# Macaron 1 with four pairs of PSUM banks, a head of products before each group's downs, and token sums on VectorE

## The chip, the cores and the metric

The kernel runs on one core of a Trainium2 chip. The metric is device time in microseconds, the median of several runs. Inside the core, TensorE (PE) multiplies and accumulates into PSUM, VectorE (DVE), ScalarE (ACT) and GpSimd (POOL) work on SBUF and PSUM, and the SP queue issues nearly all loads. PSUM has eight banks of 512 fp32 columns on 128 partitions.

## The reference

One layer of a hybrid trunk with D = 1024, 512 latent tokens x and 256 context tokens ctx (768 token columns), fp32:

```
u = rms_norm(s, g) * (1 + scale) + shift
s = s + 0.5 * gate * ((silu(u @ w_gate) * (u @ w_up)) @ w_down)      # macaron 1
... input projection; Hyena long convolution and differential attention; output projection, gated residual ...
... the same half-step once more (macaron 2); final rms_norm; out: x
```

w_gate and w_up are 1024 x 2816, w_down 2816 x 1024. Shift, scale and gate come from silu(c) @ ada_w + ada_b (9 vectors of 1024, for c and, in the first stages, for c_ctx).

## The kernel before

All large products run as three TensorE products of split operands: x = hi + lo, hi a copy rounded to fp32r and lo the rest; hi·hi + hi·lo + lo·hi (`mm3`, L252 to L255). So each weight and each activation needs a cast on ACT (hi) and a subtraction on DVE (lo). Tokens lie along the columns (TT = 768, HT = 384 is half of them), features along the partitions.

`macaron1` (L592) does the first half-step. Its 2816 hidden features are 22 f-tiles of 128. The first NP0 = 4 f-tiles are multiplied plainly (banks g0x and u0x, 768 columns in a pair of banks); Silu on ACT (L624), multiply on DVE (L625), split. The other 18 are worked on in pairs, by a scheme of the Strassen kind: a unit is the gate (m = 0) or the up matrix (m = 1) of one pair of f-tiles, and seven products j = 0 to 6 in place of eight, each of 4 x 3 = 12 matmuls with 384 columns (`product`, L731), into four accumulators: two bank pairs, called ab and cd. The weights of products 1, 2, 3 and 6 are sums of blocks (`sums_of`, L714), those of the tokens are the sums t1 to t4, made once by `token_sums` (L639; subtractions in L645) during the downs of group 0. `after_product` (L744) empties the accumulators: u is product 0 saved, further additions (L755, L760, L764, L774 to L779) give the four quarters, m = 0 ends in Silu, m = 1 in the multiply and in the split for the downs.

f-tiles come in groups (GROUPS1). After each group the downs: for each of 8 output tiles d one product with 512 latent columns and one with 256 context columns, each of 3 matmuls per f-tile, added to the stream s by DVE (`after_down`, L804). The context downs of the last group are done later, one by one between other work (the part of `macaron1` after its `yield`).

`order` is the list of all products and downs. Each step i runs its matmuls, then casts the weights of step i + 8 (9 slots; `cast` L721, `low` L726), empties the step before, and moves on something else: during group 0's downs the token sums, otherwise steps of `ada_steps` (L325), paced by PACE. These steps accumulate the later modulation vectors on DVE (L337, L339: a 128 x 1024 block of ada_w times a column of c, 70 and more of them); `ada_sum` then sums over partitions by transposing on PE (L319) and reducing on DVE (L320), and `finish_mods` (L260 to L266) adds the bias. Some steps lie between the first four f-tiles (`side`).

PSUM is one pool for the whole program: two pairs (tag "two") and four single banks ("one", downs and modulation sums). The tile framework orders each engine's instructions by the order of the code, with priorities; buffers are waited for when they come round. SP issues the loads in program order into two raw blocks of 1 MB.

```
t = bank1(f"dn0{g}{d}{strm}")[:, :n]                                        # L798
PACE = {"p": 0.2, 2: 0.35, 4: 1.6}                                          # steps per product, per down of 2 or 4 f-tiles
```

## Time and profile before

| | |
|---|---|
| three runs | 1353.21, 1356.2, 1358.03 us; median 1356.2 |
| the profiled execution | 1357.22 us, of which the span is 1355.5 |
| busy: PE / DVE / ACT / POOL | 1259.9 / 952.3 / 506.4 / 208.0 us |
| macaron 1 from the end of u03 to the last group's context downs | 144.40 to 611.08 us |

The span runs from the first to the last instruction on the core; the time of a run also has what lies around it. An engine's busy time is the sum of its instructions, where PE's overlap in a pipeline (a matmul's duration is longer than the distance to the next one's start). A wait is idle time of an engine put down to the instruction that released it.

### The profile page before, as it was taken

How to read it: one execution, taken by the hardware profiler on the slowest of the kernel's cores; microseconds unless marked ns; L12 is line 12 of the kernel's file. 1: busy time of each engine (PE TensorE's matmuls, PEld its weight loads, DVE VectorE, ACT ScalarE, POOL GpSimd, SP SyncE). 2: the span in 40 equal slices, each digit the busy share in tenths (PEclk: the TensorE clock that was granted, in tenths of full speed). 3: DMA queues.
4: the chain of work that ended last, by engine and by line, in shares of the span. 5: the costliest groups of instructions: out<-in, count | busy, mean ns of one | idle time of the engine just before them, and what ended most of it. 6: DMA issues, size and time to landing. Idle time of an engine off the chain costs nothing. (4 is left out here: it accounts for less than half of the span.)

```text
span 1355.5 us, 17492 instructions
## 1 busy us (share of the span) xinstructions
PE 1259.9 (93%) x6928; PEld 1107.7 (82%) x6928; DVE 952.3 (70%) x1453; ACT 506.4 (37%) x805; POOL 208.0 (15%) x180
## 2 busy tenths in 40 slices
PE   5899899999999999998988999888899999999996
PEld 2479788999999989987877998777788888888886
DVE  6988999778968986758598567897874333333346
ACT  5652232341331332434333345575442232222233
POOL 3630200000000000010035156464110000000001
PEclk8899899999999999999999999899899999999999
DMA  7636133222425551221412111202462322322321
GB/s 284 228 117 224 42 100 118 93 94 78 141 93 159 173 196 44 82 93 35 150 63 94 64 48 53 88 32 93 140 221 79 123 90 84 118 89 82 125 63 63
DMA packets 28370, 147.69 MB, mean 109 GB/s; under 512 B 3264, under 2 KB 3648, under 8 KB 17792
## 3 DMA queue, kind: packets, MB, share of 16 engines
q1 hardware_dynamic: 26432, 140.28, 30.9%
q0 software_dynamic: 1856, 6.29, 1.3%
q8 instruction: 54, 0.88, 0.3%
q14 instruction: 28, 0.23, 0.0%
HBM read 141.32 MB, written 5.24 MB: 108 GB/s over the span
## 5 line engine op out<-in xcount | busy, mean ns | idle before, releaser
L239 DVE TENSOR_TENSOR arena_r<-arena_f,arena_r 128x1024 fp32r<-128x1024 f32 (+5 forms) x201 | 210.8, 1059 | 156.2 <-ACT arena_r L238 153.0
L238 ACT CAST arena_r<-arena_f 128x1024 fp32r<-128x1024 f32 (+5 forms) x215 | 186.6, 879 | 353.8 <-PE gu L254 126.9
L721 ACT CAST arena_r<-arena_f 128x512 fp32r<-128x512 f32 (+1 forms) x174 | 105.8, 610 | 273.4 <-PE dn L254 102.3
L254 PE MATMUL gu<-arena_r 128*128 128x512 f32 (+1 forms) x416 | 155.5, 374 | 2.6 <-POOL arena_r L390 2.4
L253 PE MATMUL gu<-arena_r 128*128 128x512 f32 (+1 forms) x416 | 155.3, 375 | 0.7 <-ACT arena_r L238 0.6
L255 PE MATMUL gu<-arena_r 128*128 128x512 f32 (+1 forms) x416 | 155.2, 373 | 0.6 <-DVE arena_r L239 0.6
L726 DVE TENSOR_TENSOR arena_r<-arena_f,arena_r 128x512 fp32r<-128x512 f32 (+1 forms) x174 | 118.7, 686 | 34.3 <-ACT arena_r L721 32.7
L741 PE MATMUL cd<-arena_r 128*128 128x384 f32 x684 | 124.4, 335 | 5.3 <-DVE arena_f L779 5.3
L741 PEld LDWEIGHTS cd<-arena_r 128*128 128x128 f32 x684 | 118.6, 188 | 7.2 <-DVE arena_f L779 7.0
L253 PE MATMUL dn<-arena_r,arena_r 128*128 128x256 f32 (+1 forms) x328 | 107.6, 335 | 8.8 <-DVE arena_f L320 6.0
L239 POOL TENSOR_TENSOR arena_r<-arena_f,arena_r 128x1024 fp32r<-128x1024 f32 (+1 forms) x14 | 31.3, 2246 | 497.3 <-ACT arena_r L238 496.3
L254 PE MATMUL dn<-arena_r,arena_r 128*128 128x256 f32 (+1 forms) x328 | 107.6, 332 | 0.0
L255 PE MATMUL dn<-arena_r,arena_r 128*128 128x256 f32 (+1 forms) x328 | 107.1, 330 | 0.0
L339 DVE SCALAR_TENSOR_TENSOR arena_f<-arena_f,cs 128x1024 f32<-128x1024 f32 x70 | 90.4, 1302 | 10.7 <-DMA arena_f<-in_ada 10.4
L254 PEld LDWEIGHTS gu<-arena_r 128*128 128x128 f32 x416 | 80.0, 192 | 16.5 <-POOL arena_r L390 2.8
L253 PEld LDWEIGHTS gu<-arena_r 128*128 128x128 f32 x416 | 79.6, 192 | 15.6 <-issue 1.2
L741 PE MATMUL ab<-arena_r 128*128 128x384 f32 x492 | 91.0, 336 | 0.6 <-ACT arena_r L721 0.6
L255 PEld LDWEIGHTS gu<-arena_r 128*128 128x128 f32 x416 | 79.9, 192 | 13.8 <-DVE arena_r L239 0.8
L741 PEld LDWEIGHTS ab<-arena_r 128*128 128x128 f32 x492 | 85.6, 189 | 1.0 <-ACT arena_r L721 0.9
L253 PE MATMUL dn<-arena_r 128*128 128x512 f32 (+1 forms) x232 | 85.7, 370 | 0.0
L254 PE MATMUL dn<-arena_r 128*128 128x512 f32 (+1 forms) x232 | 85.7, 369 | 0.0
L255 PE MATMUL dn<-arena_r 128*128 128x512 f32 (+1 forms) x232 | 85.6, 369 | 0.0
(291 smaller groups left out, 2675.5 us busy)
## 6 DMA issues: line engine op xcount, KB each, us to landing
arena_f<-in_wgu SPq DMA_DIRECT2D x46, 1024.0 KB, 5.1
arena_f<-in_ada SPq DMA_DIRECT2D x62, 512.0 KB, 3.8
arena_f<-in_wd SPq DMA_DIRECT2D x11, 1024.0 KB, 5.1
arena_f<-in_win SPq DMA_DIRECT2D x10, 1024.0 KB, 4.9
arena_f<-in_wout SPq DMA_DIRECT2D x8, 1024.0 KB, 4.9
arena_e<-in_ada SPq DMA_DIRECT2D x10, 512.0 KB, 7.1
arena_f<-in_wd SPq DMA_DIRECT2D x4, 896.0 KB, 4.6
arena_f<-in_wd SPq DMA_DIRECT2D x4, 768.0 KB, 4.2
```

The costliest lines, as they stand in the source:

```text
L238: S.copy(hi, src)
L239: eng.tensor_tensor(out=lo, in0=src, in1=hi.bitcast(F32), op=ALU.subtract)
L253: T.matmul(out_, lh, rh, start=start, stop=False)
L254: T.matmul(out_, lh, rl, start=False, stop=False)
L255: T.matmul(out_, ll, rh, start=False, stop=stop)
L339: V.scalar_tensor_tensor(out=acc, in0=w, scalar=sc, in1=acc, op0=ALU.mult, op1=ALU.add)
L721: S.copy(slots[i % NS][0][:, :src.shape[1]], src)
L726: V.tensor_tensor(out=l, in0=src, in1=h.bitcast(F32), op=ALU.subtract)
L741: T.matmul(o, w[:, k, :], b[:, k, :], start=j < 4 and k + n == 0, stop=k == 3 and n == 2, skip_group_check=True)
```

## The change

PSUM is divided anew three times: two pairs and four singles until the first four f-tiles are done (ps0), four pairs for the rest of the stage (ps1), two and four again after it (ps2). A pool is closed before the next is opened, so the first tiles of the next wait for the readers of the former. Downs use a pair for both segments; a group of two f-tiles does two outputs per step, with weight units of two. Modulation sums use a pair, eight transposes and one reduction, and are placed earlier by a priority. The groups are (4, 4, 2, 4, 4, 4). Ahead of each group's downs stand two products of the next group (one for group 0). The second pair of a unit is now called dc, and the last two additions are one operation on 768 elements. The token sums are all on DVE. Modulation steps are paced by an estimate of DVE's spare time in each step (`spare`, COST). Down weights of group g < 5 load as 512 KB units into halves of one raw block.

```diff
-GROUPS1 = (4, 2, 4, 4, 4, 4)
-PACE = {"p": 0.2, 2: 0.35, 4: 1.6}
+GROUPS1 = (4, 4, 2, 4, 4, 4)
+COST = {"p": 2.1, "d": 4.2, "w": 0.69, "post": ((0, .55, .55, .55, 0, 0, .95), (0, .55, .55, 1.1, .55, 0, 3.8)),
+        "dn": 1.23, "mod": 1.3}
+HEAD = 2
+AHEAD = 300
+MOD_STEPS = 120
...
-    ps = ctx.enter_context(tc.tile_pool(name="ps", bufs=1, space=PSUM))
+    banks = {"n": (2, 4)}
+    def new_banks(name, *n):
+        if "ctx" in banks:
+            banks["ctx"].close()
+        banks["ctx"], banks["n"] = ExitStack(), n
+        banks["ps"] = banks["ctx"].enter_context(tc.tile_pool(name=name, bufs=1, space=PSUM))
+    new_banks("ps0", 2, 4)
     def bank2(name):
-        return ps.tile([P, 1024], F32, tag="two", name=name, bufs=2)
+        return banks["ps"].tile([P, 1024], F32, tag="two", name=name, bufs=banks["n"][0])
...
-        for half in range(2):
-            pt = bank1(f"ada_ps{j}_{st}{half}")
-            for n in range(4):
-                T.transpose(pt[:, n * P:(n + 1) * P], acc[:, (4 * half + n) * P:(4 * half + n + 1) * P], ident)
-            V.tensor_reduce(out=red[:, 4 * half:4 * half + 4], in_=pt.rearrange("p (n k) -> p n k", k=P),
-                            axis=AX.X, op=ALU.add)
-        finish_mods(j, st, red)
+        with tc.high_priority(offset=AHEAD):
+            pt = bank2(f"ada_ps{j}_{st}")
+            for n in range(KT):
+                T.transpose(pt[:, n * P:(n + 1) * P], acc[:, n * P:(n + 1) * P], ident)
+            V.tensor_reduce(out=red, in_=pt.rearrange("p (n k) -> p n k", k=P), axis=AX.X, op=ALU.add)
+            finish_mods(j, st, red)
...
             side(f)
+        new_banks("ps1", 4, 0)
...
-                sub(G, z, p12[1], p11[1])
-                sub(V, x, p12[0], p11[0])
-                sub(G, y, p22[0], p12[0])
-                sub(V, x, x, z, ALU.add)
+                sub(x, p12[0], p11[0])
+                sub(z, p12[1], p11[1])
+                sub(x, x, z, ALU.add)
...
+        for g, nf in enumerate(GROUPS1):
+            add_products(g, len(todo[g]))
+            if g < len(GROUPS1) - 1:
+                add_products(g + 1, HEAD if g else 1)
+            n_d, step = 8 // nf, 4 // nf
+            for d in range(0, KT, step):
...
         def product(g, pr, m, j, slot):
             if j == 0:
-                st["ab"], st["cd"] = bank2(f"ab{g}{pr}{m}"), bank2(f"cd{g}{pr}{m}")
-            at = (0, 1, 2, 3, 0, 2, 3)[j]
-            o = st["cd" if at > 1 else "ab"][:, 512 * (at % 2):512 * (at % 2) + HT]
+                st["ab"] = st["dc"] = bank2(f"ab{g}{pr}{m}")
+            if j == 2:
+                st["dc"] = bank2(f"dc{g}{pr}{m}")
+            at = (0, 1, 3, 2, 0, 3, 2)[j]
+            o = st["dc" if at > 1 else "ab"][:, 512 * (at % 2):512 * (at % 2) + HT]
...
-            elif j == 5:
-                add(1, 0, pc_, st["u"])
+            elif j == 6:
+                o = w if m else act[:, 1:3, :]
+                V.tensor_tensor(out=o, in0=dc.rearrange("p (b w) -> p b w", b=2)[:, :, :HT],
+                                in1=st["u"].unsqueeze(1).to_broadcast([P, 2, HT]), op=ALU.add)
+                out(act[:, 1:3, :], o)
...
-        def down(g, nf, d, slot, seg):
+        def down(g, nf, d, slot, seg, bank):
             t0, n, strm = seg
-            t = bank1(f"dn0{g}{d}{strm}")[:, :n]
+            t = bank[:, t0:t0 + n]
...
+        def spare(i):
+            kind, arg, _ = order[i]
+            if kind == "d" and arg[0] in (0, len(GROUPS1) - 1):
+                return 0.0
+            t = COST[kind] - (COST["post"][arg[2]][arg[3]] if kind == "p" else COST["dn"] * (4 // arg[1]))
+            if i + LA < n:
+                t -= COST["w"] * (1 + len(source(i + LA)[1]))
+            return t
+        share = COST["mod"] * MOD_STEPS / sum(map(spare, range(n)))
+        def pace(t, sums):
+            paced[0] += t * share / COST["mod"]
+            while paced[0] >= 1 and (sums or paced[1] != "sum"):
...
+            if pending:
+                pending()
             ahead = i + LA
             if ahead < n:
                 cast(ahead)
                 sums_of(ahead + 1)
-            if pending:
-                pending()
-            if ahead < n:
                 low(ahead)
...
-                pace(PACE["p" if kind == "p" else arg[1]])
+                pace(spare(i), kind == "d" or arg[3] in (2, 5))
...
         R.put(*u_b, *[b for x in t_b for b in x])
+        new_banks("ps2", 2, 4)
         yield
         for i in range(n - KT, n):
             g, nf, d, _ = order[i][1]
-            after_down(down(g, nf, d, slots[i % NS], SEG_C), d, SEG_C)
+            after_down(down(g, nf, d, slots[i % NS], SEG_C, bank2(f"dnc{d}")), d, SEG_C)
...
-        for _ in range((2, 6, 6, 4)[f]):
+        for _ in range((3, 6, 6, 3)[f]):
```

In the pieces of the order below, a row is one instruction (xN: N in a row) with its line, what it writes and what it reads; arena_r, arena_r2 and arena_f are the buffers in SBUF, a name with digits of a tile ahead of its running number (u03 is the up tile of f-tile 3, ab100 and dc100 the pairs of group 1, pair 0, m = 0, dn00 the down of group 0, d = 0; ada_ps2_0 the sum of modulation 2 for the latent stream). Lines of the changed kernel are its own: L270 to L272 is mm3, L336 the transposes, L337 the reduction, L780 the products.

The first place is PE at the end of the four plain f-tiles. Before:

```order
L254 MATMUL u03_997<-arena_r_85 128x256
L255 MATMUL u03_997<-arena_r_85 128x256
L319 MATMUL ada_ps2_00_1101<-ident_65,arena_f_84 128x128 x4
L319 MATMUL ada_ps2_01_1107<-ident_65,arena_f_84 128x128 x4
L319 MATMUL ada_ps2_10_1115<-ident_65,arena_f_84 128x128 x4
L319 MATMUL ada_ps2_11_1121<-ident_65,arena_f_84 128x128 x4
L741 MATMUL ab100_1430<-arena_r_85 128x384 x3
L253 MATMUL dn0000_1148<-arena_r2_646,arena_r_85 128x512
L254 MATMUL dn0000_1148<-arena_r2_646,arena_r_85 128x512
```

In the changed kernel the transposes stand inside u03, of which this is the second half:

```order
L270 MATMUL u03_999<-arena_r_85 128x512
L271 MATMUL u03_999<-arena_r_85 128x512
L336 MATMUL ada_ps2_1_1113<-ident_65,arena_f_84 128x128 x8
L272 MATMUL u03_999<-arena_r_85 128x512
L270 MATMUL u03_999<-arena_r_85 128x512
```

and at its end:

```order
L270 MATMUL u03_999<-arena_r_85 128x256
L271 MATMUL u03_999<-arena_r_85 128x256
L272 MATMUL u03_999<-arena_r_85 128x256
L780 MATMUL ab100_1150<-arena_r_85 128x384 x12
L270 MATMUL dn00_1171<-arena_r2_646 128x512
L271 MATMUL dn00_1171<-arena_r2_646 128x512
```

The two sums have moved from behind u03 into it (ada_ps2_0 some seven rows earlier), and twelve matmuls of ab100 stand ahead of the first down, where three stood.

The second place is DVE at the same point of the program. Before (L645 are token sums, L726 low halves of weights, L625 the multiply of u03, L320 the reductions):

```order
L239 TENSOR_TENSOR arena_r_85<-arena_f_84,arena_r_85 128x768
L645 TENSOR_TENSOR arena_f_84<-arena_r_85,arena_f_84 128x768
L645 TENSOR_TENSOR arena_f_84<-arena_f_84,arena_r_85 128x768
L726 TENSOR_TENSOR arena_r_85<-arena_f_84,arena_r_85 128x512
L625 TENSOR_TENSOR arena_f_84<-u03_997,arena_f_84 128x768
L320 TENSOR_REDUCE arena_f_84<-ada_ps2_00_1101 128x4
L320 TENSOR_REDUCE arena_f_84<-ada_ps2_01_1107 128x4
L239 TENSOR_TENSOR arena_r2_646<-arena_f_84,arena_r2_646 128x768
L260 TENSOR_TENSOR mod_81<-arena_f_84,prm_63 128x8
```

And in the changed kernel (L763 are low halves of weights, L640 the multiply of u03, L337 the reductions, L353 and L355 modulation steps, L663 token sums):

```order
L763 TENSOR_TENSOR arena_r_85<-arena_f_84,arena_r_85 128x512
L337 TENSOR_REDUCE arena_f_84<-ada_ps2_0_1101 128x8
L353 TENSOR_SCALAR arena_f_84<-arena_f_84,cs_77 128x1024
L277 TENSOR_TENSOR mod_81<-arena_f_84,prm_63 128x8
L355 SCALAR_TENSOR_TENSOR arena_f_84<-arena_f_84,cs_77 128x1024
L337 TENSOR_REDUCE arena_f_84<-ada_ps2_1_1113 128x8
L283 TENSOR_SCALAR hg_83<-mod_81 128x8
L353 TENSOR_SCALAR arena_f_84<-arena_f_84,cs_77 128x1024
L277 TENSOR_TENSOR mod_81<-arena_f_84,prm_63 128x8
L355 SCALAR_TENSOR_TENSOR arena_f_84<-arena_f_84,cs_77 128x1024
L283 TENSOR_SCALAR hg_83<-mod_81 128x8
L763 TENSOR_TENSOR arena_r_85<-arena_f_84,arena_r_85 128x512
L640 TENSOR_TENSOR arena_f_84<-u03_999,arena_f_84 128x768
L355 SCALAR_TENSOR_TENSOR arena_f_84<-arena_f_84,cs_77 128x1024
L256 TENSOR_TENSOR arena_r2_646<-arena_f_84,arena_r2_646 128x768
```

The reductions stand ahead of u03's multiply now and behind it before; the multiply stands right behind a low half of a weight, and no token sum but the first stands ahead of it.

The third place is PE at the end of a group. Before, the end of group 2's last unit and the first down of group 2:

```order
L741 MATMUL ab211_2170<-arena_r_85 128x384 x24
L741 MATMUL cd211_2171<-arena_r_85 128x384 x24
L741 MATMUL ab211_2170<-arena_r_85,arena_r2_646 128x384 x12
L741 MATMUL cd211_2171<-arena_r_85,arena_r2_646 128x384 x12
L741 MATMUL cd211_2171<-arena_r_85 128x384 x12
L253 MATMUL dn0200_2290<-arena_r2_646,arena_r_85 128x512
L254 MATMUL dn0200_2290<-arena_r2_646,arena_r_85 128x512
```

In the changed kernel, the end of group 1's last unit and the first down of group 1 (dn10):

```order
L780 MATMUL dc111_1820<-arena_r_85 128x384 x24
L780 MATMUL ab111_1785<-arena_r_85 128x384 x12
L780 MATMUL ab200_1902<-arena_r_85 128x384
L780 MATMUL dc111_1820<-arena_r_85 128x384 x24
L780 MATMUL ab200_1902<-arena_r_85 128x384 x11
L780 MATMUL ab200_1902<-arena_r_85,arena_r2_646 128x384 x12
L270 MATMUL dn10_1941<-arena_r2_646 128x512
L336 MATMUL ada_ps3_0_1968<-ident_65,arena_f_84 128x128 x8
L271 MATMUL dn10_1941<-arena_r2_646 128x512
L272 MATMUL dn10_1941<-arena_r2_646 128x512
```

Before, the last product of the unit is followed by the down that reads it. Now 24 matmuls of group 2's first unit (ab200) stand between them, and the transposes of a modulation sum stand inside the first down.

## Rows read from the trace of the kernel before

**Rows 1.** The page, part 1: busy us, share of the span, instructions of each engine.

```profile
PE 1259.9 (93%) x6928; PEld 1107.7 (82%) x6928; DVE 952.3 (70%) x1453; ACT 506.4 (37%) x805; POOL 208.0 (15%) x180
```

**Rows 2.** The trace in windows: length, busy (instructions) per engine, granted clock PEclk, DMA share, GB/s.

```profile
150.00:175.00 25.00, 22.14 (x109) 19.02 (x110) 24.08 (x34) 5.97 (x9) 8.01 (x4) 0.86 0.12 43
175.00:200.00 25.00, 24.11 (x143) 22.32 (x142) 25.00 (x38) 7.51 (x13) 0.00 (x0) 1.00 0.32 96
200.00:225.00 25.00, 22.14 (x118) 21.00 (x119) 24.54 (x36) 7.98 (x17) 0.00 (x0) 0.96 0.59 200
225.00:250.00 25.00, 25.00 (x141) 22.85 (x140) 21.26 (x37) 7.84 (x13) 0.00 (x0) 0.97 0.13 43
250.00:400.00 150.00, 147.44 (x850) 142.00 (x849) 118.54 (x186) 53.30 (x91) 0.00 (x0) 1.00 0.32 106
400.00:600.00 200.00, 195.91 (x1123) 184.83 (x1123) 155.38 (x244) 65.35 (x109) 5.24 (x2) 1.00 0.37 121
```

**Rows 3.** Waits of PE, 100 to 660 us: who, for whom, total us, times, longest.

```profile
PE cd L741 <- DVE arena_f L779: 7.0, 7, 2.1
PE dn L253 <- DVE arena_f L320: 6.0, 1, 6.0
PE dn L253 <- ACT arena_r L238: 2.8, 2, 1.8
PE ab L741 <- ACT arena_r L721: 0.6, 1, 0.6
```

**Rows 4.** Timeline of PE: start, duration, instruction, idle before and its releaser.

```profile
144.40 1.91 PE L319 MATMUL ada_ps<-ident,arena_f 128*128 128x128 f32 x16
146.06 0.77 PE L741 MATMUL ab<-arena_r 128*128 128x384 f32 x3
152.86 0.79 PE L253 MATMUL dn<-arena_r,arena_r 128*128 128x512 f32 x1 [6.02 <-DVE arena_f L320]
...
259.53 4.32 PE L741 MATMUL cd<-arena_r 128*128 128x384 f32 x24
263.69 2.25 PE L741 MATMUL ab<-arena_r 128*128 128x384 f32 x12
...
607.22 0.39 PE L254 MATMUL dn<-arena_r 128*128 128x512 f32 x1
...
611.08 0.28 PE L253 MATMUL dn<-arena_r,arena_r 128*128 128x256 f32 x1
...
612.39 0.28 PE L255 MATMUL dn<-arena_r,arena_r 128*128 128x256 f32 x1
```

**Rows 5.** Waits of DVE, 146 to 600 us.

```profile
DVE arena_r L726 <- ACT arena_r L721: 29.6, 35, 1.4
DVE arena_f L804 <- PE dn L255: 21.3, 23, 2.5
DVE arena_f L339 <- DMA arena_f<-in_ada: 9.3, 9, 2.3
```

**Rows 6.** Timeline of DVE, low halves of weights.

```profile
129.43 2.49 DVE L726 TENSOR_TENSOR arena_r<-arena_f,arena_r 128x512 fp32r<-128x512 f32 x4
...
160.40 2.15 DVE L726 TENSOR_TENSOR arena_r<-arena_f,arena_r 128x512 fp32r<-128x512 f32 x1
```

**Rows 7.** Groups of DVE by line and shape, 146 to 600 us: busy, mean ns, idle.

```profile
L726 DVE TENSOR_TENSOR arena_r<-arena_f,arena_r 128x512 fp32r<-128x512 f32 x160 | 111.6, 700 | 31.2 <-ACT arena_r L721 29.6
L339 DVE SCALAR_TENSOR_TENSOR arena_f<-arena_f,cs 128x1024 f32<-128x1024 f32 x49 | 62.5, 1280 | 9.5 <-DMA arena_f<-in_ada 9.3
...
L804 DVE SCALAR_TENSOR_TENSOR arena_f<-dn,hg,arena_f 128x512 f32<-128x512 f32 x43 | 32.1, 747 | 15.1 <-PE dn L255 14.7
...
L779 DVE TENSOR_TENSOR arena_f<-cd,arena_f 128x384 f32<-128x384 f32 x18 | 9.9, 550 | 0.0
...
L645 DVE TENSOR_TENSOR arena_f<-arena_f,arena_r 128x768 f32<-128x768 f32 x4 | 3.8, 947 | 0.0
```

**Rows 8.** Timeline of GpSimd, one of the token sums.

```profile
160.15 1.84 POOL L645 TENSOR_TENSOR arena_f<-arena_r 128x768 f32<-128x768 f32 x1 [3.98 <-DVE arena_f L645]
```

More of the change, by code (lines that the diff above doesn't have):

```diff
@@ L672, in macaron1, with add_products @@
         units, order = [], []
[L673 removed]
+        f0 = 0
+        todo = {}
         for g, nf in enumerate(GROUPS1):
[L675 to L682 removed]
+            todo[g] = [(g, pr, m, j, (f0 - NP0) // 2 + pr) for pr in range(nf // 2 if g else 0)
+                       for m in range(2) for j in range(7)]
+            f0 += nf
+        def add_products(g, n):
+            for g, pr, m, j, at in todo[g][:n]:
+                if j == 0:
+                    units.append((a["wgu1"][at, m], m, 0))
+                    st["u"] = len(units) - 1
+                order.append(("p", (g, pr, m, j), st["u"]))
+            del todo[g][:n]
+        st, f0 = {}, 0
+        for g, nf in enumerate(GROUPS1):
[4 more added lines that the diff above has]
+            for d in range(0, KT, step):
                 if d % n_d == 0:
                     at = f0 * P * D + d * nf * P * P
[L685 removed]
+                    units.append((a["wd1"][at:at + 1024 * P].rearrange("(p x) -> p x", p=P),
+                                  int(g < len(GROUPS1) - 1), d // n_d % 2))
                 order.append(("d", (g, nf, d, d % n_d), len(units) - 1))
@@ L691, in load, with raw @@
             if u < len(units):
-                raws[u] = r_raw.next()
-                nc.sync.dma_start(raws[u].v(2048)[:, :units[u].shape[1]], units[u])
+                src, i, half = units[u]
+                w = src.shape[1]
+                raws[u] = r_raw.blocks[i].v(2048)[:, 1024 * half:1024 * half + w]
+                nc.sync.dma_start(raws[u], src)
+        def raw(u):
+            return raws.get(u, r_raw.blocks[0].v(2048))
         s_r = [A.get(512) for _ in range(2)]
@@ L717, in cast @@
             u = order[i][2]
-            if i == 0 or order[i - 1][2] != u:
+            if u + 1 not in raws and (order[i][0], units[min(u + 1, len(units) - 1)][0].shape[1]) != ("d", 2048):
                 load(u + 1)
@@ L742, in product, with after_product, out @@
                              skip_group_check=True)
-        def after_product(g, pr, m, j, banks):
-            pa, pb, pc_, pd = [banks[i // 2][:, 512 * (i % 2):512 * (i % 2) + HT] for i in range(4)]
-            act = [b.v(2, HT) for b in act_b.blocks]
+        def after_product(g, pr, m, j, ab, dc):
+            pa, pb, pd, pc_ = [x[:, 512 * i:512 * i + HT] for x in (ab, dc) for i in range(2)]
+            act = act_b.v(4, HT)
             ah, al = acts[g]
-            def out(i, t, src=None):
-                o = act[i][:, t, :]
+            def out(o, src):
                 if m == 0:
-                    S.activation(o, o if src is None else src, AF.Silu)
+                    S.activation(o, src, AF.Silu)
                 else:
                     V.tensor_tensor(out=o, in0=src, in1=o, op=ALU.mult)
-            def add(i, t, p, q):
-                if m == 0:
-                    V.tensor_tensor(out=act[i][:, t, :], in0=p, in1=q, op=ALU.add)
-                    out(i, t)
-                else:
-                    w = st["w_r"].next().v(HT)
-                    V.tensor_tensor(out=w, in0=p, in1=q, op=ALU.add)
-                    out(i, t, w)
-            if "u_r" not in st:
-                st["u_r"], st["w_r"] = Ring(A, 2, HT), Ring(A, 2, HT)
-            u_r, w_r = st["u_r"], st["w_r"]
+            w = w_b.v(2, HT)
             if j == 0:
@@ L811, in macaron1 @@
             low(i)
-        sums, paced = token_sums(), [0.0]
+        sums, paced = token_sums(), [0.0, ""]
         pending, n = None, len(order)
-        def pace(share):
-            paced[0] += share
-            while paced[0] >= 1:
+        def spare(i):
[10 more added lines that the diff above has]
+            while paced[0] >= 1 and (sums or paced[1] != "sum"):
                 paced[0] -= 1
-                next(steps, None)
+                paced[1] = next(steps, "")
+                sums = False
         for i, (kind, arg, u) in enumerate(order):
@@ L834, in macaron1 @@
                     pending = None
-                ts = [(down(g, nf, d, slot, seg), d, seg) for seg in ((SEG_L,) if last else (SEG_L, SEG_C))]
+                ts = []
+                for e in range(d, d + 4 // nf):
+                    bank = bank2(f"dn{g}{e}")
+                    ts += [(down(g, nf, e, slot, seg, bank), e, seg) for seg in ((SEG_L,) if last else (SEG_L, SEG_C))]
                 post = lambda ts=ts: [after_down(*x) for x in ts]
+            if pending:
+                pending()
             ahead = i + LA
@@ L873, in dit_layer @@
     spec = filter_spectrum()
[L874 removed]
+    act_b = A.get(2 * TT, 10816)
     with tc.tile_pool(name="early", bufs=1) as early:
```

88 lines of the change are left out of this document (38 added, 50 removed).

## The prediction

> **What bounds the kernel now.** I read the busy shares first, then the stage in windows, then the waits of PE with its timeline, then DVE: its waits, its groups by shape, and its rows where GpSimd works beside it.
>
> PE is busy for 93% of the span [rows 1], so the end moves only by what PE does not lose any more. The change touches the stage from the first modulation sum after u03, at 144.40, to the first context-token down product of the last group, at 611.08 [rows 4]: 466.7 us. Its PE work has a fixed price at full clock, from starts in the timeline: 24 matmuls of 384 columns take 263.69 - 259.53 = 4.16 us, 0.173 each; 17 of 512 columns 611.08 - 607.22 = 3.86, 0.227 each; 11 of 256 columns 612.39 - 611.08 = 1.31, 0.119 each; 16 transposes 1.66, 0.104 each. The code issues 1512, 528, 432 and 72 of them: 262.0 + 119.9 + 51.5 + 7.5, about 441 us (441.5 with the unrounded pitches). PE thus loses 25.2 us in this stage, and the change can win no more than that.
>
> The waits name 16.4 of it [rows 3]: 7.0 where a second bank pair waits for DVE's last addition of the unit before (L779), 6.0 once at the first down product, 2.8 where downs wait for the high half of a split (L238), 0.6 for a weight cast. The windows show the second part [rows 2]: the granted clock falls to 0.86 in 150:175 and to 0.96 and 0.97 in the two windows around 225. [...] The 6.0 us wait ends inside it, at 152.86; about 5.5 us lie behind it and cost half, 2.7. [...]
>
> DVE is the engine that PE waits for. It is busy 24.08, 25.00 and 24.54 of 25 us in 150:225, only 79% of 250:400, and it waits itself for casts and for PE [rows 5]. Its work is enough to fill one part of the stage and too little to fill the rest.
>
> **The change, part by part.**
>
> *Start of the stage.* Before, 16 transposes stand between u03 and product ab100, three matmuls of it run, and dn0000 waits until 152.86 because the banks of the sums are read late: on DVE their reductions (L320) stand behind u03's multiply [rows 4]. Now each sum uses one bank pair, its eight transposes stand inside u03's own products, its single reduction stands on DVE ahead of u03's multiply, and a whole product (12 x 0.173 = 2.1 us) stands ahead of the downs. New is a pool switch: ab100 may not start before all readers of the first pool's banks are done, u03's multiply among them. That multiply stands behind the low half of a weight whose slot comes free when u03's last matmul ends: 0.6 + 0.95 us of DVE and the handing over, 2.2 us of PE. In u03 itself the transposes wait for the Silu that frees their pair, which stands in ACT's queue behind casts: 1.3 us. I take 3.5; if both are covered 1.1 (the low half alone), if DVE is as late as before, 7. The wait that cost 6.0, and 2.7 of low clock behind it, goes.
>
> *Four pairs of banks.* A unit (gate or up of one f-tile pair) needs two pairs. With two in all, the next unit's second pair waits for the last addition of this one (the 7.0). With four it does not: the readers have a whole unit, 7 x 2.1 = 14.6 us, more time. The last two additions become one operation on 768 elements, 0.95 for 2 x 0.55 [rows 7], ordered so that banks come free in the order of need. All 7.0 goes.
>
> [...]
>
> *Products ahead of the downs.* Two products of the next group (4.2 us of PE) stand between the last product of a group and its first down, which waits for a split (multiply, cast, low half: some 0.95 us for each of three operations of 768). That covers the 2.8. The group of two f-tiles now comes third; there a down reads both f-tiles at once and its steps do two outputs, so I leave 1.0 there.
>
> *Token sums off GpSimd.* Six operations move to DVE, 6 x 0.87 = 5.2 us (0.947 each, less the 0.08 by which starts run closer than durations, as 0.69 and 0.60 of the low halves below) [rows 7]. Taken off is what DVE lost beside them: a low half of a weight took 2.15 us against 0.70, started 0.25 us after a GpSimd sum of 1.84 [rows 6 to 8]; six such rows add up to 6.9 us over their groups' means. Net -1.7 on DVE. The phase is still nearly full: 42 us of DVE rows against 33 of downs plus the head product; t2 to t4 come 2 to 4 us ahead of need.
>
> [...]
>
> *Modulation steps paced by DVE's spare time.* They are drawn to the front: the remaining ones are all placed by the downs of group 3, some 60% of the stage. Over groups 1 to 3 DVE then has 83 low halves and 37 weight sums at 0.60 (four low halves start to start in 129.43's row: (2.49 - 0.69)/3 = 0.60), 45 accumulations at 1.19, 41 additions of 384 at 0.47, 26 operations of 768 at 0.87, 16 down evacuations at 0.66 + 0.40 (512 and 256 columns; 128 columns more cost 0.13 by the additions of 384 and 512), six reductions of 1024 elements at 1.12 (estimate, by the same 0.13 from 0.60) and 5 first terms at 0.66 [rows 6, 7]: 72 + 53.6 + 19.3 + 22.6 + 17 + 6.7 + 3.3, about 195 us. PE has there 71 products of 2.08, 12 down steps of 4.16 and 6 sums of 0.87: 203 us. That is 96%. From group 4 on it is about 70%. A queue at 96% has little room for DVE's own waits, which were 60 us in 146:600 [rows 5]; but most of those are waits of an idle engine that is early. In 150:225 DVE was 98% busy, so it can be filled. I take 2.5 us of PE; the ends are 0, and 30 if the waits stay.
>
> *End of the stage and smaller edits.* A second pool switch ahead of the context downs, 1.2 us (one evacuation and its handing over), and two pairs for them in place of four single banks, 0.5. Weight units of 512 KB in halves of one block, the side steps (3, 6, 6, 3), and the sum of the modulations inside the second FFN cost nothing: SP issues them further ahead than they land, PE's instruction count stays at 6879 matmuls and the later order is the same. If a load is late, its cast is, and the cost shows as the 0.6 row does.
>
> **Sum.** Lost after: start 3.5, boundary 1.0, DVE 2.5, end 1.7, small gaps 2.5 (of 4.4; some were at the places that go): 11.2 against 25.2, a gain of 14.0. The profiled execution took 1357.2 for a span of 1355.5; so 1343.2. It lies 1.0 above the median of 1356.2: 1342.
>
> **Rivals.**
> 1. *PE nearly gapless.* DVE never late; start 1.1, boundaries 0, end 0.5, gaps 2: lost 4, gain 21, 1335. For it: waits on L779 vanish whole, and the stretch 225:250 shows 25.00 of 25 busy. Against it: 96% demand on DVE. 0.18.
> 2. *New waits eat half.* The pool switch costs its 7, the clock falls behind it as it did at 152.86 (2.7), sums drawn ahead hold up PE's queue two or three times: lost 18, gain 7, 1349. 0.17.
> 3. *No change.* DVE's lateness is what the waits carry; with banks enough it arrives at the next consumer, a product whose weight's low half is late. [...] Against it: the average of DVE over the stage is about 82%. 0.08.
> 4. *Slower: DVE starves PE in groups 1 to 3.* The steps drawn ahead are not paid back. DVE was idle for 22% of the time between 250 and 600 [rows 2], 44 us in a stretch of 203; if most of that (its waits on casts, on in_ada and on PE), 38, survives while the demand is 195, DVE needs 233 for what PE does in 203, and PE waits 30. Less the 20 saved elsewhere: +10, 1366. It decides from the point where DVE's idle time in groups 1 to 3 exceeds what its 8 us of slack plus the 20 saved can carry, about 28 us. Against it: the 98% of 150:225. 0.07.
>
> **How the numbers follow.** The forecast has 0.50, with its own range 1337 to 1348 (start 1.1 to 7, DVE 0 to 6). What this kernel's runs can tell from no change is 0.3%, 4.1 us. Faster by more, below 1352.1: 0.50, 0.18, and 0.15 of the 0.17 of rival 2, together 0.83. Same: the rest of rival 2, 0.08 of rival 3 and a little of rival 4: 0.11. Slower: 0.06. The range leaves out rival 4, most of rival 3 and the low end of rival 1: 1333 to 1353.
>
> **What would show it.** Right: no PE wait on the evacuation of the unit's last addition; the first down of group 0 starts near 152 behind a whole product; PEclk 1.00 in every window from 150 on; DVE 96% or more from about 190 to 390 and then under 80%; no low half of a weight above 1 us in 150:175. Wrong: PE waiting for lows of weights or for sums of weights in groups 1 to 3 by more than 6 us in all (rivals 3, 4), a wait over 5 us at ab100 or at the first context down (rival 2), or a fall of the clock behind either.

## The result, and the profile after

The changed kernel takes 1338.0 us (median of 4 runs, 1335.84 to 1340.09) against 1357.1 of the kernel before (4 runs): ratio 0.986, 95% interval 0.9827 to 0.9893, 19 us faster. The forecast was 1342. The profiled execution took 1336.8 us, span 1335.0, 20.5 less than before. In the experiments below one execution of e3_tokens and one of e4_head0 took over 4340 us, for a reason that is not known, and is left out of their times.

The page's first part and the windows answer to [rows 1, 2]:

```profile
PE 1254.1 (94%) x6928; PEld 1102.9 (83%) x6928; DVE 944.3 (71%) x1418; ACT 503.6 (38%) x792; POOL 196.1 (15%) x174
```

```profile
150.00:175.00 25.00, 25.00 (x142) 22.04 (x142) 24.04 (x34) 8.60 (x13) 0.00 (x0) 1.00 0.33 106
175.00:200.00 25.00, 25.00 (x150) 24.02 (x149) 24.80 (x39) 9.56 (x15) 0.00 (x0) 1.00 0.09 31
200.00:225.00 25.00, 25.00 (x146) 25.00 (x145) 24.99 (x37) 11.53 (x20) 0.00 (x0) 1.00 0.37 122
225.00:250.00 25.00, 25.00 (x149) 24.45 (x148) 24.55 (x35) 9.58 (x16) 0.00 (x0) 1.00 0.55 179
250.00:400.00 150.00, 149.34 (x871) 141.05 (x870) 145.29 (x209) 46.17 (x77) 0.00 (x0) 1.00 0.53 169
400.00:600.00 200.00, 199.16 (x1129) 187.28 (x1128) 128.35 (x197) 65.73 (x106) 4.80 (x2) 1.00 0.21 69
```

PE is busy without a gap from 150 to 250, the granted clock is 1.00 throughout, and DVE, 97% busy up to 400 (145.29 of 150) where it was 79%, keeps up. PE's waits between 100 and 640 [rows 3], and four rows of its timeline [rows 4]:

```profile
PE hy_ps L272 <- DVE arena_r L256: 3.0, 1, 3.0
PE dnc L270 <- DVE arena_f L832: 2.8, 3, 1.3
PE ab L780 <- DVE arena_f L640: 1.6, 1, 1.6
PE ada_ps L336 <- ACT arena_f L639: 0.7, 1, 0.7
...
PE dn L271 <- DVE arena_r L256: 0.3, 1, 0.3
PE dc L780 <- DVE arena_f L806: 0.2, 1, 0.2
```

```profile
136.15 0.40 PE L270 MATMUL u<-arena_r 128*128 128x512 f32 x1
...
149.03 2.35 PE L780 MATMUL ab<-arena_r 128*128 128x384 f32 x12 [1.61 <-DVE arena_f L640]
151.22 0.39 PE L270 MATMUL dn<-arena_r 128*128 128x512 f32 x1
...
593.11 0.39 PE L270 MATMUL dnc<-arena_r,arena_r 128*128 128x256 f32 x1 [0.84 <-DVE arena_f L832]
```

The 7.0 us of the second pair are 0.2, the 2.8 of the downs 0.3. From u03's first matmul (136.06 before, 136.15 now) to the first context down (611.08, 593.11) the stage took 475.0 us and takes 457.0: 18.1 less. From there to the last matmul of the sums of squares (ms_b) it is 1.6 longer (66.0, 67.6), from that to the last y_ps 6.1 shorter (89.7, 83.6), and the rest 2.1 longer (1.6 of it in attention, with other places of low clock: 0.93 in all four windows of 50 us from 800 to 1000, where before it was 1.00, 0.93, 0.93 and 0.90). That 6.1 was in no step of the forecast. It lies 120 us behind the stage, at v_ps. PE and DVE before, then after:

```profile
742.66 0.58 PE L254 MATMUL v_ps<-arena_r 128*128 128x256 f32 x1 [4.92 <-DVE arena_r L239]
```

```profile
737.31 0.93 DVE L1041 TENSOR_TENSOR arena_f<-arena_f 128x256 f32<-128x256 f32 x1 [1.55 <-POOL arena_f L1039]
...
740.96 1.64 DVE L239 TENSOR_TENSOR arena_r<-arena_f,arena_r 128x1024 fp32r<-128x1024 f32 x1
```

```profile
719.44 0.38 PE L271 MATMUL v_ps<-arena_r 128*128 128x256 f32 x1 [0.44 <-DVE arena_r L256]
```

```profile
715.13 3.12 DVE L1199 TENSOR_TENSOR arena_r<-arena_f,arena_r 64x768 fp32r<-64x768 f32 x1
718.18 1.21 DVE L256 TENSOR_TENSOR arena_r<-arena_f,arena_r 128x1024 fp32r<-128x1024 f32 x1
```

Before, the low half of a v weight (L239) stands behind four operations, one waiting for GpSimd; after, it follows the query split (L1199) at once.

### The profile page after: what moved, and what is told of

The parts are those of the page before. It is cut to its first block, busy times and chain, and to the rows that moved or that the text cites. A ratio compares the mean times of both kernels' runs of the same rounds, so it can differ in the third digit from the quotient of the medians.

```text
span 1335.0 us, 17439 instructions
## 1 busy us (share of the span) xinstructions
PE 1254.1 (94%) x6928; PEld 1102.9 (83%) x6928; DVE 944.3 (71%) x1418; ACT 503.6 (38%) x792; POOL 196.1 (15%) x174
## 5 line engine op out<-in xcount | busy, mean ns | idle before, releaser
L256 DVE TENSOR_TENSOR arena_r<-arena_f,arena_r 128x1024 fp32r<-128x1024 f32 (+5 forms) x201 | 205.9, 1034 | 157.2 <-ACT arena_r L255 154.0
L758 ACT CAST arena_r<-arena_f 128x512 fp32r<-128x512 f32 x170 | 105.3, 621 | 270.6 <-PE dn L271 98.0
L270 PE MATMUL gu<-arena_r 128*128 128x512 f32 (+1 forms) x416 | 155.2, 374 | 0.9 <-ACT arena_r L255 0.7
L272 PE MATMUL gu<-arena_r 128*128 128x512 f32 (+1 forms) x416 | 155.0, 373 | 0.6 <-DVE arena_r L256 0.6
L763 DVE TENSOR_TENSOR arena_r<-arena_f,arena_r 128x512 fp32r<-128x512 f32 x170 | 118.4, 703 | 25.2 <-ACT arena_r L758 23.1
L780 PE MATMUL dc<-arena_r 128*128 128x384 f32 x636 | 116.1, 335 | 0.2 <-DVE arena_f L806 0.2
L271 PE MATMUL dn<-arena_r,arena_r 128*128 128x256 f32 (+1 forms) x336 | 111.3, 332 | 0.3 <-DVE arena_r L256 0.3
L780 PEld LDWEIGHTS dc<-arena_r 128*128 128x128 f32 x636 | 110.4, 188 | 0.8 <-DVE arena_f L806 0.6
L270 PE MATMUL dn<-arena_r,arena_r 128*128 128x256 f32 (+1 forms) x336 | 110.8, 332 | 0.0
L272 PE MATMUL dn<-arena_r,arena_r 128*128 128x256 f32 (+1 forms) x336 | 110.7, 330 | 0.0
L780 PE MATMUL ab<-arena_r 128*128 128x384 f32 x504 | 93.0, 334 | 1.6 <-DVE arena_f L640 1.6
L270 PEld LDWEIGHTS gu<-arena_r 128*128 128x128 f32 x416 | 79.4, 191 | 16.1 <-issue 1.2
L272 PEld LDWEIGHTS gu<-arena_r 128*128 128x128 f32 x416 | 79.9, 192 | 13.9 <-DVE arena_r L256 0.8
L355 DVE SCALAR_TENSOR_TENSOR arena_f<-arena_f,cs 128x1024 f32<-128x1024 f32 x70 | 88.6, 1281 | 3.5 <-DMA arena_f<-in_ada 3.1
L780 PEld LDWEIGHTS ab<-arena_r 128*128 128x128 f32 x504 | 87.7, 188 | 1.8 <-DVE arena_f L640 1.8
L832 DVE SCALAR_TENSOR_TENSOR arena_f<-dn,hg,arena_f 128x512 f32<-128x512 f32 x88 | 52.4, 626 | 35.6 <-PE dn L272 35.2
L271 PE MATMUL dn<-arena_r 128*128 128x512 f32 (+1 forms) x192 | 73.0, 380 | 0.1
L272 PE MATMUL dn<-arena_r 128*128 128x512 f32 (+1 forms) x192 | 72.7, 378 | 0.0
```

The source lines that it names most:

```text
L256: eng.tensor_tensor(out=lo, in0=src, in1=hi.bitcast(F32), op=ALU.subtract)
L270: T.matmul(out_, lh, rh, start=start, stop=False)
L271: T.matmul(out_, lh, rl, start=False, stop=False)
L272: T.matmul(out_, ll, rh, start=False, stop=stop)
L355: V.scalar_tensor_tensor(out=acc, in0=w, scalar=sc, in1=acc, op0=ALU.mult, op1=ALU.add)
L758: S.copy(slots[i % NS][0][:, :src.shape[1]], src)
```

## The experiments

Stage is the stretch of 475.0 and 457.0 us above, counted from u03's first matmul, from one profiled execution each; it is read beside the time, since the granted clock over the span differs between executions (of the changed kernel's four, 0.974 at 1340.1 us to 0.981 at 1336.8 us). How far a stage can be off by chance: the changed kernel, e9 and e7, whose code is the same up to the end of the stage, have 457.0, 456.8 and 456.1. The ratio is to runs of the kernel before made beside the run; the changed kernel has 0.986 (0.9827 to 0.9893). The intervals of e2, e10 and e1b overlap that one, though each of their single runs (1341.74 us and more) is slower than each of the changed kernel's (at most 1340.09). All but e8 start from the changed kernel. Undone alone were not: the addition on 768 elements, the order of the groups, and the 512 KB units.

| run | edit | time us | ratio to before (95%) | stage us |
|---|---|---|---|---|
| e9_addr | buffers behind the stage at their old addresses | 1343.2 | 0.9913 (0.9895 to 0.9932) | 456.8 |
| e2_ahead0 | no priority for the sums | 1342.2 | 0.9907 (0.9888 to 0.9925) | 461.4 |
| e8_before_sums | before + that priority | 1361.6 | 1.0041 (1.0028 to 1.0055) | 466.7, u03 starting 9.1 us later than before |
| e10_zy | two buffers of the token sums exchanged | 1345.4 | 0.9911 (0.9883 to 0.994) | 463.1 |
| e1_banks | two pairs and four singles | 1353.4 | 0.9977 (0.9956 to 0.9997) | 464.2 |
| e1b_banks | same, early sums on a pair | 1344.2 | 0.9911 (0.9883 to 0.9939) | 461.1 |
| e3_tokens | token sums on GpSimd | 1350.0 | 0.9944 (0.9927 to 0.9961) | 462.2 |
| e4_head0 | no heads, weights of some products overwritten | 1347.0 | 0.9935 (0.9911 to 0.9958) | 467.0 |
| e4b_head0 | no heads, four units of down weights not loaded | 1350.7 | 0.9957 (0.9941 to 0.9973) | 468.2 |
| e5_pace | old pacing | 1338.8 | 0.9866 (0.9848 to 0.9884) | 456.7 |
| e6_steps240 | steps drawn ahead twice as fast | 1395.7 | 1.029 (1.0263 to 1.0317) | 511.3 |
| e7_dnc1 | context downs on singles | 1335.6 | 0.9849 (0.9828 to 0.9869) | 456.1 |

**Buffers behind the stage.** Among blocks that fit, the arena hands out the one that has been free longest, so other buffers in the stage move those behind it. PLACES is a list of the 157 addresses that the kernel before used there, one for each `get`.

```diff
     def get(self, words, at=None):
+        if self.replay:
+            at = self.replay.pop(0)
...
         new_banks("ps2", 2, 4)
+        A.replay = list(PLACES)
```

> The changed kernel with the buffers of the stage after macaron 1 (hyena and attention) at the addresses in SBUF that the kernel before gave them; nothing else. On DVE the low half of the first v weight then stands behind the filter additions and a query split again, as before. If the 4.9 us wait of v_ps for that low half in the profile of before came from this order, it returns (4 to 5 us, and with it a fall of the clock worth up to 3): 1342 to 1346. Rival: the wait was an accident of one execution; then 1337 to 1339 and no such wait.

The order on DVE and the wait are back, and ms_b to y_ps takes 89.8 us as before (83.6 to 83.9 in every other run from the changed kernel):

```profile
729.74 0.58 PE L277 MATMUL v_ps<-arena_r 128*128 128x256 f32 x1 [4.92 <-DVE arena_r L262]
```

About a quarter of the gain in time (5.1 of 19 us) comes from addresses.

**The start: are the sums the cause?**

```diff
-AHEAD = 300
+AHEAD = 0
```

> The changed kernel without the priority for the modulation sums (offset 0 in place of 300): the transposes stand behind u03 again, the reductions behind u03's multiply, as before the change. If the sums read late were the cause of the 6.0 us wait at the first down, it returns with its clock fall: the first down near 155 to 158 in place of 151.2, time about 1345. Rival: DVE was late then because token sums and weights stood ahead of u03's multiply; here nothing of that stands ahead, so u03's multiply starts near 147, the two reductions add 1.2 to 2.5, the first product starts near 150.2 in place of 149.0, the first down near 152.4, time 1338 to 1341.

```diff
-        for half in range(2):
...
-        finish_mods(j, st, red)
+        with tc.high_priority(offset=300):
+            for half in range(2):
...
+            finish_mods(j, st, red)
```

> The kernel before with one part of the change alone: the modulation sums get the priority (offset 300), in their old form on two single banks. If the sums were the cause of the 6.0 us wait, it goes, with the 2.7 us of low clock behind it: 6 to 9 us faster, 1348 to 1351. Rival, DVE late behind token sums: the first down starts some 8 us earlier (144.5) but waits for the split of f-tile 3 after nine matmuls, since u03's multiply still comes at about 151; the wait is renamed, gain 0 to 2 us, 1355 to 1357.

PE's timeline and one of its waits in e2, then its timeline in e8:

```profile
149.31 2.37 PE L780 MATMUL ab<-arena_r 128*128 128x384 f32 x12 [2.04 <-DVE arena_f L337]
...
151.52 0.39 PE L270 MATMUL dn<-arena_r 128*128 128x512 f32 x1
```

```profile
PE dn L270 <- ACT arena_r L255: 2.0, 1, 2.0
```

```profile
125.45 1.94 PE L320 MATMUL ada_ps<-ident,arena_f 128*128 128x128 f32 x8 [6.57 <-DVE arena_f L340]
...
153.42 0.28 PE L255 MATMUL u<-arena_r 128*128 128x256 f32 x1
153.54 0.40 PE L253 MATMUL dn<-arena_r,arena_r 128*128 128x512 f32 x1
```

Without the priority the first down starts at 151.5 in place of 151.2: in the changed kernel the order of the sums is not needed to keep the 6.0 us away. Its 4.4 us of stage lie elsewhere, most at the group of two f-tiles (a wait of 2.0 at a down, and a fall of the clock to 0.83 in 310:320). In the kernel before, the priority alone makes it slower, in a way that neither theory had: single banks are free early, so the transposes move up to where PE waits 6.6 us, and 9.8 in all, for the accumulations that they read. In the changed kernel the pair, still held by f-tile 3's gate, keeps them back. In e8 the first down does follow u03 at once, without the 6.0 us, but u03 ends 9.1 us later than before, and the first down starts at 153.5 in place of 152.9. So the wait has only moved ahead of u03; since DVE gained 9 us on PE by it, e8 can't tell whether the place of the sums alone, or DVE's lateness, made the 6.0. What else was late then? DVE before, then after:

```profile
143.87 0.95 DVE L645 TENSOR_TENSOR arena_f<-arena_r,arena_f 128x768 f32<-128x768 f32 x1
...
149.78 0.96 DVE L645 TENSOR_TENSOR arena_f<-arena_f,arena_r 128x768 f32<-128x768 f32 x1
...
151.25 0.95 DVE L625 TENSOR_TENSOR arena_f<-u,arena_f 128x768 f32<-128x768 f32 x1
```

```profile
147.41 0.69 DVE L763 TENSOR_TENSOR arena_r<-arena_f,arena_r 128x512 fp32r<-128x512 f32 x1 [1.74 <-PE u L271]
148.02 0.95 DVE L640 TENSOR_TENSOR arena_f<-u,arena_f 128x768 f32<-128x768 f32 x1
```

Before, token sums and their splits fill DVE up to u03's multiply at 151.25, 6.7 us behind u03's end. After, DVE waits for PE there: z, in which the sums begin, has moved into the block that this multiply fills, so they cannot come ahead of it.

```diff
-            x, z = act_b.v(4, HT)[:, 0:2, :], act_b.v(4, HT)[:, 2:4, :]
+            x, y = act_b.v(4, HT)[:, 0:2, :], act_b.v(4, HT)[:, 2:4, :]
...
-            y = w_b.v(2, HT)
+            z = w_b.v(2, HT)
```

> The changed kernel with two buffers of the token sums exchanged: z, in which t1 begins, is the free block w_b, and y the second half of the activation block that the multiply of f-tile 3 writes. In the changed kernel it is the other way round, so that every token subtraction but one had to come behind f-tile 3's multiply. On DVE eight token subtractions and two low halves now stand ahead of that multiply, as in the kernel before. If this is what made DVE late at the start of the stage, the first product starts about 6 us later after the end of u03 (7 to 9 us behind u03's last matmul in place of 1.9), with a fall of the clock, 1343 to 1347. Rival: the first wait was the late 1 MB unit of down weights and GpSimd, and this changes the start by less than 1.5 us: 1337 to 1340.

The size came (first down 5.0 us later counted from u03's start, stage +6.1, time +7.4), at another place than expected: PE's timeline and ACT's.

```profile
140.99 1.97 PE L336 MATMUL ada_ps<-ident,arena_f 128*128 128x128 f32 x8 [4.28 <-ACT arena_f L639]
```

```profile
138.88 0.83 ACT L255 CAST arena_r<-arena_f 128x768 fp32r<-128x768 f32 x1 [3.01 <-DVE arena_f L663]
...
140.14 0.80 ACT L639 ACTIVATE arena_f<-g 128x768 f32<-128x768 f32 x1
```

The cast of a token sum now stands ahead of the Silu that frees the pair, and the transposes wait for it inside u03. The first product started only 1.5 us behind u03's last matmul, where 7 to 9 were expected: DVE was not late at the multiply here. So in the changed kernel the placing of the token sums decides the start, by the choice of a buffer. That they also made the 6.0 us of the kernel before is argued from DVE's rows there; no run of that kernel shows it.

**Four pairs of banks.** e1 and e1b, where the transposes ahead of u03 keep a pair:

```diff
-        new_banks("ps1", 4, 0)
+        new_banks("ps1", 2, 4)
...
-            t = bank[:, t0:t0 + n]
+            t = bank1(f"dn{g}{d}{strm}")[:, :n]
...
-                    bank = bank2(f"dn{g}{e}")
+                    bank = None
```

In both the sums in the stage go to single banks in halves, with two reductions of half the width.

> The changed kernel with the bank layout of before in the Strassen part: two pairs and four single banks, downs and modulation sums on singles; heads, fused addition, token sums on DVE and pacing are kept. If the four pairs as such take away the 7.0 us wait of a unit's second pair for the last addition of the unit before, that wait returns: 5 to 12 us in all at the first matmul into dc, since DVE is fuller now in groups 1 to 3, time about 1345 (1342 to 1350). Rival: the fused last addition and the earlier evacuations already take it away, then under 2 us of such waits and 1338 to 1340.

> As e1_banks (two pairs and four singles in the Strassen part), but with the two modulation sums that stand inside u03 on a pair, so that their transposes keep their place in PE's order. From the first product to the last unit the trace of e1_banks took 426.0 us against 416.9 of the changed kernel; if that is what the banks are worth, 8 to 10 us come back here, 1346 to 1348, spread over waits of dc for the last addition and one fall of the clock, and the start stays at 149. Rival: part of the 9 us was a consequence of the late start; then under 5 us.

e1 mixed two things: its sums on single banks ran into the wait of e8 (5.2 us, ahead of u03). e1b keeps them in place; its waits of PE in the stage:

```profile
PE dc L788 <- DVE arena_f L814: 1.3, 3, 0.6
PE ab L788 <- DVE arena_f L809: 1.2, 1, 1.2
PE ab L788 <- ACT arena_f L800: 1.2, 2, 0.6
...
PE dc L788 <- DVE arena_r L256: 0.3, 1, 0.3
```

The banks, with the sums in the form that they force, are worth 4.2 us of stage (461.14 - 456.96): under the 5 of the rival, and less than the 7.0 that the wait was. That the fused addition keeps the other part away is likely, but it was not undone alone.

**Token sums.** Three subtractions per half go to GpSimd:

```diff
-            def sub(o, p, q, op=ALU.subtract):
+            def sub(o, p, q, op=ALU.subtract, eng=V):
...
-                V.tensor_tensor(out=o, in0=p, in1=q, op=op)
+                eng.tensor_tensor(out=o, in0=p, in1=q, op=op)
...
-                sub(z, p12[1], p11[1])
+                sub(z, p12[1], p11[1], eng=G)
...
-                sub(z, p22[0], p12[0])
-                sub(y, p22[1], p12[1])
+                sub(z, p22[0], p12[0], eng=G)
+                sub(y, p22[1], p12[1], eng=G)
```

> The changed kernel with the six token subtractions that were on GpSimd put there again. By the prediction's term DVE loses 6.9 us beside GpSimd for 5.2 us saved, 1.7 net, in a phase with 2 to 4 us to spare: 0 to 3 us of PE at the first products of group 1 (waits on t1 to t4), 1338 to 1341. Rival: GpSimd chains are longer than that (two of the subtractions now follow each other there, 1.8 to 2.5 us each), t3 comes late in each half and PE loses 4 us or more. Other rival: the saved 5.2 us decide and it is 2 us faster.

Stage +5.3, but 1.3 of it lies within u03, where none of these subtractions runs: the transposes there waited 1.9 us for the Silu in place of 0.7, since ACT waited longer for down weights. The other 4.0 are nearer to the rival's 4 than to 1.7, though not by its mechanism: neither DVE nor PE waits for GpSimd there. DVE was full in 175 to 200 (25.00 of 25), and PE waited for u's first addition, which it does not in the changed kernel. GpSimd, DVE and PE there:

```profile
159.94 2.23 POOL L663 TENSOR_TENSOR arena_f<-arena_r 128x768 f32<-128x768 f32 x1 [2.70 <-DVE arena_f L663]
```

```profile
161.05 1.94 DVE L256 TENSOR_TENSOR arena_r<-arena_f,arena_r 128x768 fp32r<-128x768 f32 x1
```

```profile
196.78 2.73 PE L780 MATMUL ab<-arena_r 128*128 128x384 f32 x14 [2.15 <-DVE arena_f L801]
```

Beside GpSimd the low half took 1.94 us, against 0.95 alone; [rows 6, 8] show the same with 2.15. The low half ended 0.8 us after the subtraction beside it, about its own length. Six DVE rows beside GpSimd are 5.8 us longer than their like, for 5.2 us saved: a net of 0.6 on DVE, where the prediction had 1.7. The other 7 us of e3's time lie outside the stage and were not traced to a cause.

**Heads.** No products of the next group ahead of a group's downs:

```diff
-                add_products(g + 1, HEAD if g else 1)
+                add_products(g + 1, 0)
...
```

In e4_head0 the last up unit of a group read down weights in two of its four blocks; in e4b the first down unit of groups 1 to 4 was not loaded and these downs used what was in the block. The edit above leaves out the conditions that order the loads. The number of products and downs is the same.

> The changed kernel without products ahead of the downs, with the weight loads in an order that fits this (e4_head0 loaded down weights over products' weights, so part of its products were computed with other weights). Stage from u03's first matmul to the context downs 457.0 us in the changed kernel. If the heads take away the waits for the split, it becomes 460 to 464, the waits at the first downs of groups 1 to 4, 0.7 to 2 us each, most at the group of two f-tiles; time 1341 to 1345. Rival: under 1.5 us, 1337 to 1340.

```profile
139.83 1.97 PE L336 MATMUL ada_ps<-ident,arena_f 128*128 128x128 f32 x8 [3.48 <-ACT arena_f L639]
...
316.16 1.16 PE L270 MATMUL dn<-arena_r,arena_r 128*128 128x512 f32 x3 [4.37 <-ACT arena_r L255]
```

Stage +11.2 (e4_head0, with the same expectation in substance: +10.1). Only one boundary waits long, that of the two-f-tile group, whose first down reads the f-tiles just split; with a fall of the clock behind it (from 318.09 to 319.80 matmuls of 512 columns start 0.43 us apart, 0.23 from 320.69 on) the decade from 310 lost 6.5 us. About 4 more are at the start (3.5 for the Silu ahead of the transposes, 0.7 in the changed kernel: without the product, casts of down weights that wait for their loads stand ahead of it). Neither run without heads computed with the right weights throughout, so the price is that of the order, with this flaw; the two agree within 1.1 us.

**Pacing.**

```diff
-            paced[0] += t * share / COST["mod"]
-            while paced[0] >= 1 and (sums or paced[1] != "sum"):
+            paced[0] += t
+            while paced[0] >= 1:
...
-                pace(spare(i), kind == "d" or arg[3] in (2, 5))
+                pace({"p": 0.2, 2: 0.7, 4: 1.6}["p" if kind == "p" else arg[1]], True)
```

> The changed kernel with modulation steps paced as before the change (0.2 per product, 1.6 per down of four f-tiles, 0.7 per step of the two-f-tile group), so that they reach to the last group but one in place of 60% of the stage. If the front-loading costs the 1.9 us that PE loses at 312 and 381 to 392 and buys nothing with four pairs of banks, this is 0 to 2 us faster: 1336 to 1338. If the pacing by spare time is what keeps DVE on time, downs with 1.6 steps (1.06 + 0.6 + 0.6 + 2.1 us of DVE in 4.16) push evacuations late: 3 to 6 us slower, 1341 to 1344.

```profile
250.00:400.00 150.00, 149.40 (x870) 141.53 (x869) 119.81 (x180) 46.36 (x77) 0.00 (x0) 1.00 0.29 93
400.00:600.00 200.00, 198.62 (x1137) 186.63 (x1136) 155.65 (x228) 66.48 (x107) 4.79 (x2) 1.00 0.39 126
```

DVE is 80% busy in 250:400 in place of 97% and nothing changes: the pacing neither costs nor buys anything that these runs can tell. A step further:

```diff
-MOD_STEPS = 120
+MOD_STEPS = 240
```

> The changed kernel with the modulation steps drawn ahead twice as fast (MOD_STEPS 240): all are done by the downs of group 2. By the sums of DVE's rows it then has 144.6 us of work from group 0's last down to the first down of group 2, in which PE has 121 (119.4 in the changed kernel), 24 us too many. If DVE's demand is what counts and the buffers (weights eight steps ahead, four pairs) carry some 8 to 14 us of lateness, PE loses 8 to 16 us there and gets nothing back: 1346 to 1354. Rival A: lateness passes on at once, 24 us: 1360 and more. Rival B: the buffers carry it all, under 2 us, 1338 to 1340.

54 us of stage, and a time of 1395.7: no slack carried it, and the loss is over twice the 24 of rival A. PE's row, DVE's largest wait in 200 to 350, and the windows:

```profile
295.92 1.97 PE L336 MATMUL ada_ps<-ident,arena_f 128*128 128x128 f32 x8 [12.61 <-DVE arena_f L355]
```

```profile
DVE arena_f L355 <- DMA arena_f<-in_ada: 13.4, 15, 2.4
```

```profile
250.00:300.00 50.00, 32.26 (x161) 27.81 (x160) 40.75 (x55) 7.44 (x12) 0.00 (x0) 0.76 0.58 184
300.00:350.00 50.00, 30.86 (x166) 28.36 (x165) 33.52 (x43) 6.11 (x10) 0.00 (x0) 0.80 0.56 165
```

DVE was not even full (33.5 of 50): the steps ran at the pace of their loads, two in flight, and PE stood at the transposes behind the last of them, at a granted clock of 0.76. Such waits sum to 35.8 us; my count of DVE's demand left this place out.

**End of the stage.** The context downs on single banks:

```diff
-            t = bank[:, t0:t0 + n]
+            t = bank[:, t0:t0 + n] if bank is not None else bank1(f"dnc{d}")[:, :n]
...
-            after_down(down(g, nf, d, slots[i % NS], SEG_C, bank2(f"dnc{d}")), d, SEG_C)
+            after_down(down(g, nf, d, slots[i % NS], SEG_C, None), d, SEG_C)
```

> The changed kernel with the context downs of the last group in the four single banks in place of the two pairs (the pairs serve nothing else there). If the pairs are what adds 1.6 us between the first context down and the end of the sums of squares (67.6 us against 66.0 before), it goes: waits of dnc for L832 fall from 2.8 to under 1.5 us, 1336 to 1337.5. Rival: DVE bounds that stretch and the wait moves to the next matmul, 0 to 0.5 us, 1337.5 to 1338.5.

```profile
PE hy_ps L270 <- DVE arena_f L832: 2.6, 2, 2.3
PE dnc L270 <- DVE arena_f L832: 0.8, 1, 0.8
```

The wait moves from dnc to hy_ps, as the rival has it, and the stretch to the end of the sums of squares takes 68.9 us, not less than 67.6: what makes it longer than before stays open. The time, 1335.6, is the lowest measured, but its interval (0.9828 to 0.9869) overlaps that of the changed kernel; that it is faster is not shown.

## Why the prediction was right, and where not

- **Gain 14.0, measured 18.1 in the stage, 19 in time.** Of 25.2 us lost, 7.2 are left where 11.2 were forecast: 2.9 at the start (3.5), 1.9 at the two-f-tile group and at 380 to 400 (1.0 + 2.5), 0.84 at the second pool switch (1.2), 1.5 in small gaps (2.5). Each of these was somewhat high; the end was not: behind the stage 1.6 came on top of the 0.84, 2.4 for 1.7. No row shows the 4.4 of small gaps by itself: it is what 25.2 leaves behind the 16.4 of waits and the clock's part, and for the clock the trace of the kernel before shows 0.50 over the 5.5 us behind the first down, 2.7 lost, and 0.57 from 223 to 227, 1.7 lost. The mechanism of the whole (PE's listed waits go, the low clock with them) held: the windows and the waits above. All the signs named for it came (the first down at 151.2 for 152, DVE 97% busy up to 400 and 64% after), none of those against it. The prediction's count of 6879 matmuls is on neither page; both have 6928 instructions of PE.
- **The start.** The size was right (2.9 for 3.5), and the new pool's wait is the 1.6 us at ab100. The cause given for the 6.0, the place of the reductions, was at best half of it: with them back behind u03's multiply the start is 0.3 us later (e2), with them moved alone the wait moves too (e8). Token sums ahead of that multiply cost the changed kernel 5.0 us (e10), and the prediction did not name their place as what takes the wait away; that it went all the same was partly luck. The 1.3 for the Silu came to 0.7, with ACT waiting for down weights that the prediction had landing in time.
- **Four pairs.** 7.0 went; undoing the banks alone brings 4.2 back (e1b).
- **Heads.** 2.8 was the wait of the kernel before, and it went. What the heads are worth in the changed kernel is far more: without them the stage is 11.2 longer (e4b, with the loads left out as told), most of it at the group of two f-tiles, which now comes third, and at the Silu in u03.
- **Token sums.** As work of DVE 1.7 net was too large (0.6 in e3); as time of PE, which the sum put at nothing, it is 4.0 to 5.3.
- **Pacing.** 2.5 of cost, 0 shown (e5). Rival 4 was set by DVE's idle share. The changed kernel paid nothing of it; at twice the pace (e6) its price is steeper than I had it, and it is paid at PE's transposes. Where between the two it begins, no run shows.
- **"The later order is the same" failed**: addresses moved, an order on DVE changed, and 6.1 us came of it (e9). Without them the time is 1343.2, still in the range, so the forecast does not owe its place in the range to them; but they and the 4.1 us by which the stage gained more than forecast hide 3.7 us lost behind the stage (1.6 and 2.1), of which 0.5 was foreseen.
- **The undone parts sum to 31 us** (6.1 + 4.4 + 4.2 + 5.3 + 11.2) for 18.1 gained. They overlap: several protect PE from the same late DVE, by the releasers of the waits above, and some carry others, as the heads do for the place of the two-f-tile group.
- **Clock.** With four pairs the granted clock was 1.00 in all windows from 150 to 600. How long a single wait was did not by itself tell whether the granted clock fell behind it. Behind 6.0 us before it was 0.50 for 5.5 us, with 512-column matmuls starting 0.43 us apart in place of 0.23; behind 4.3 in e10 (142.61 to 144.02), 4.4 in e4b (318.09 to 319.80) and 12.6 in e6 (297.54 to 299.39) they started 0.41 to 0.57 apart; behind 1.8 before and 2.0 in e2, both at the first down of a group, it fell to 0.83 over 10 us; behind 2.1 before and 2.2 in e3, both between products, it stayed at 1.00. The windows, in this order (before, for the two stretches of the first bullet; before, e2, before, e3):

```profile
152.86:158.36 5.50, 5.50 (x14) 4.33 (x15) 4.60 (x8) 1.04 (x2) 1.82 (x1) 0.50 0.00 0
223.00:227.00 4.00, 4.00 (x15) 3.47 (x14) 1.54 (x2) 0.33 (x1) 0.00 (x0) 0.57 0.31 128
220.00:230.00 10.00, 7.97 (x34) 6.69 (x35) 7.53 (x14) 2.98 (x5) 0.00 (x0) 0.83 0.44 180
310.00:320.00 10.00, 7.97 (x34) 6.33 (x33) 8.71 (x13) 3.53 (x6) 0.00 (x0) 0.83 0.74 253
340.00:350.00 10.00, 7.93 (x45) 7.62 (x45) 10.00 (x16) 3.40 (x6) 0.00 (x0) 1.00 0.50 156
190.00:200.00 10.00, 7.36 (x40) 6.43 (x38) 10.00 (x18) 3.84 (x7) 0.00 (x0) 1.00 0.00 0
```

## What to carry to other kernels

Before crediting an early or late instruction to an edit of its order, look which buffer it writes and who used that buffer last: here the choice of one block held token sums back and saved 5 us, and the addresses that an arena gave out later saved 6 more. A priority for work that PE does for another engine was safe here only while something held it behind the data it reads: placed ahead of them, the transposes stopped PE for 6.6 us (e8) and 12.6 us (e6). Undo parts one by one to rank them, not to add them up.

## What was not expected of the hardware

DVE's busy share did not tell whether it held PE up: it was 97% busy from 200 to 400 us in the changed kernel, where PE lost 2.7 us in all against its price at full clock, and 67% busy (33.5 of 50) from 300 to 350 in e6, where PE lost 23.
